# Reading the moving operand of the projections in another column order, with the weight buffers 128 bytes further on

## The chip, the cores and the metric

The kernel runs on one core of one Trainium2 chip. The metric is the device time in microseconds (us) of one execution of the whole program; the times shown are medians of several runs.

## The reference

One decoder block on x of 2048 rows by 1024 columns, float32. A row norm gives h; h times a 1024 x 7680 matrix gives every branch's input. One branch is a gated 31-tap depthwise convolution with a layer norm, the other a sliding-window attention (16 query heads, 4 key/value heads of 64, window 128, a sink per head). Each branch has its own gate and output matrix; two sigmoid gates merge them; a last matrix, the residual and a row norm follow.

```python
h = rmsnorm(x, norm_g[l])
proj = jnp.einsum("bsd,de->bse", h, w_in[l])
glu_in, conv_gate, q, k, v, attn_gate, merge_logits = jnp.split(proj, SPLIT_POINTS, axis=-1)
c = conformer_conv(glu_in, conv_dw_w[l], conv_dw_b[l], conv_ln_g[l], conv_ln_b[l])
y_conv = jnp.einsum("bsc,cd->bsd", c * jax.nn.silu(conv_gate), w_conv_out[l])
...
a = sliding_window_attention(q, k, v, attn_sinks[l])
y_attn = jnp.einsum("bsa,ad->bsd", a * jax.nn.silu(attn_gate), w_attn_out[l])
merged = g_conv * y_conv + g_attn * y_attn
x = x + jnp.einsum("bsd,de->bse", merged, w_out[l])
return rmsnorm(x, final_norm_g)
```

## The kernel before

The sequence is worked through in two sweeps of 1024 rows (`T`), each in two halves of 512 (`TH`). In the projections the weights stand still in TensorE and the activations move: a weight block is 1024 x 128, kept as eight tiles of 128 x 128 (`KC` = 8), and a moving tile is 128 partitions x 512 columns, one half of the rows. Each float32 operand is kept as two parts, a rounded high part and the remainder, and a product is three matmuls into the same PSUM bank: high x high, high weight x low activation, low weight x high activation. `product` (lines 299 to 302) issues these three for one of the eight tiles; `project` (line 307) calls it for two halves and eight tiles, so a weight block makes 2 x 8 x 3 = 48 matmuls. Each is issued with its own weight load (128 x 128, shown as PEld), which runs beside the matmul before it.

A sweep has 76 such blocks: 16 for the gated convolution's input (`gb`, `ga`), 8 for q, 2 for k, 2 for v, 32 for the four gates (`ag`, `cg`, `ma`, `mc`), 8 for the attention's output (`ya`) and 8 for the convolution's (`yc`). Between them, in an order that the kernel itself writes out by a running estimate of TensorE's time (class `Line`; `MM_US` is its price of a matmul), lie the small matmuls of the attention: scores (`sc`, line 799), transposes (`tpp`, line 834) and the products with v (`ov`, line 858), 64 blocks of each. Two matmul sums for the layer norm (`lnmu`, `lnvar`, line 918) use a constant matrix `ones` as weights. The last product with `w_out` (`o`, line 1199) does not go through `product`: there the activations stand still and the weights move.

TensorE runs its instructions in that written order; VectorE (DVE), ScalarE (ACT) and GpSimd (POOL) each run theirs in program order. SyncE (SP) issues all DMAs.

Where the operands lie in SBUF matters for what is changed. In each partition the constants come first, then `slots`, a row of named buffers of 4096 bytes (three of them 4608) made by `slot` (line 82), then `stage`, the buffers of 2048 bytes for raw weights and for their high and low parts (`whi`, `wlo`; lines 262 and 274 to 275), then `work`. The moving tiles `hT`, `aT`, `uT` and `u` are slots. A slot gets its place when it is first used, and `a12` is used last of all. In the program before, every slot and every stage buffer starts at a multiple of 512 bytes, so each weight tile row (128 x 4 = 512 bytes) and each moving row (512 x 4 = 2048 bytes) does too. The matrix `ones` starts 224 bytes behind such a multiple, and the moving tiles of `lnmu` and `lnvar`, which are `work` buffers, 96 bytes behind one. The first two weight blocks of all lie in slots, not in `stage` (`home`, line 409).

Of the kernel before, what the change touches and what calls it, by code (L numbers as in the profile page):

```python
# [19 lines left out]
P = 128  # L20
S = 2048
D = 1024
KC = D // P
# [31 lines left out]
def hybrid_block(ctx: ExitStack, tc: tile.TileContext, x, xt, par_d, w_in, w_conv, sinks, w_attn, w_out,  # L55
                 fin_g, rope_t, out):
    nc = tc.nc
    pe, act, dve, pool = nc.tensor, nc.scalar, nc.vector, nc.gpsimd
# [21 lines left out]
    WIDE = {"c6", "c7", "a14"}  # L80

    def slot(tag, shape, dt, name):
        n = int(np.prod(shape[1:]))
        full = 1024 + P if tag in WIDE else 1024
        t = slots.tile([P, full], dt, tag=tag, name=name)
        v = t[:, 0:n]
        if len(shape) == 3:
            v = v.rearrange("p (a b) -> p a b", b=shape[2])
        elif len(shape) == 4:
            v = v.rearrange("p (a b c) -> p a b c", b=shape[2], c=shape[3])  # L90
        return v
# [20 lines left out]
    ident_r = const.tile([P, P], F32R, name="ident_r")  # L112
    ident = f(ident_r)
    ident_0 = slot(A[4], [P, P], F32, "ident_0")
    make_identity(nc, ident_0)
    dve.tensor_copy(out=ident_r, in_=ident_0)
    ones_0 = slot(A[5], [P, P], F32, "ones_0")
    dve.memset(ones_0, 1.0 / D)
    ones = const.tile([P, P], F32R, name="ones")
# [146 lines left out]
    def load_w(src, name, home=None, steps=None, raws=None):  # L266
# [29 lines left out]

        return lambda k: (parts[k // 4][0][:, k % 4, :], parts[k // 4][1][:, k % 4, :]), keep

    def product(ps, w, r, k, order=(0, 1, 2)):
        parts = ((w[0], r[:, 0, :]), (w[0], r[:, 1, :]), (w[1], r[:, 0, :]))  # L300
        for i, (a, b) in enumerate(parts[n] for n in order):
            pe.matmul(out=ps, lhsT=a, rhs=b, start=(k == 0 and i == 0), stop=(k == KC - 1 and i == 2))  # L302

    def small_bank(name):
        return tp_ps.tile([P, 4, P], F32, tag="tp", name=name).rearrange("p a b -> p (a b)")
# [1 line left out]
    def project(src, rhs, name, evac, halves=(0, 1), small=False):  # L307

        got = {}

        def early():
            got["raws"] = [fetch_raw(src, name, kh) for kh in range(2)]

        def prefetch():
            got["w"] = load_w(src, name, raws=got.get("raws"))

        prefetch.early = early

        def blocks():
            for half in halves:  # L320
                if small:
                    ps = small_bank(f"mm_{name}{half}")
                else:
                    ps = mm_ps.tile([P, TH], F32, tag="mm", name=f"mm_{name}{half}")
                for k in range(KC):
                    product(ps, got["w"][0](k), rhs(k, half), k)
                    if k == KC - 1:
                        with tc.high_priority(offset=PRIO):
                            evac(half, ps)
                    if half == halves[-1] and k % 4 == 3:  # L330
                        got["w"][1](k // 4)
                    yield 3 * MM_US

        return prefetch, blocks, (src, name, evac)
# [8 lines left out]
    def make_tiles(tags, half, name):  # L343
        return [slot(tags[half * 8 + k], [P, 2, TH], F32R, f"{name}{half}_{k}") for k in range(KC)]
# [46 lines left out]
    def opening(items):  # L391
# [58 lines left out]
        def first_blocks():  # L450
            for half in range(2):
                for i in range(2):
                    name = f"mm_{parts[i][1]}0{half}"
                    ps[i, half] = (small_bank(name) if half and i else
                                   mm_ps.tile([P, TH], F32, tag="mm", name=name))
                for k in range(KC):
                    scaled_split(u[half][k], raw[half][k], k)
                    for i in range(2):
                        product(ps[i, half], ws[i][0](k), u[half][k], k, (0, 2, 1))
                        yield 3 * MM_US  # L460
            squares(0)
# [9 lines left out]
        def later(i, half):  # L471
            def blocks():
                name = f"mm_{parts[i][1]}0{half}"
                b = small_bank(name) if half == 0 else mm_ps.tile([P, TH], F32, tag="mm", name=name)
                for k in range(KC):
                    product(b, ws[i][0](k), u[half][k], k)
                    yield 3 * MM_US
                    if i == 2 and k == (2, 4)[half]:
                        yield spread(half)
                        if half == 0:  # L480
                            squares(1)
                        if half:
                            for j in range(2):
                                for kh in range(2):
                                    ws[j][1](kh)
                leave(i, half, b)
                if half:
                    for kh in range(2):
                        ws[i][1](kh)
                if half == 0 and i == 3:  # L490
                    ht[0] = make_tiles(h_tags[0], 0, "hT0_")
                    for k in range(KC):
                        put_h(ht[0][k], raw[0][k], rs[:, 0], k)
                if half == 1 and i == 2:
                    ht[1] = make_tiles(h_tags[0], 1, "hT0_")
                    for k in range(KC):
                        put_h(ht[1][k], raw[1][k], rs[:, 1], k)

            return blocks
# [777 lines left out]
```

## Time and profile before

| what | value |
|---|---|
| median of 3 runs | 1992.11 us (1991.31 to 1993.75) |
| the profiled execution: its own time | 1991.75 us |
| its span, first to last instruction | 1990.0 us |
| mean granted TensorE clock | 0.999 |
| TensorE matmuls (PE) | 1976.9 us busy, 9264 of them |
| weight loads (PEld) | 1649.1 us, 9264 |
| VectorE, ScalarE, GpSimd | 1309.2, 982.7, 429.9 us |
| DMA | 386.13 MB, mean 194 GB/s |

Read the busy time of PE with care: matmuls overlap one another in the records (one of 512 columns is shown with 389 ns, yet the next begins earlier than that), so the distance from start to start tells what one costs. The chain of work that ended last does this sum: each of its pieces is a run of instructions with its length and count, and length divided by count is the time of one.

### The profile page before, as it was taken

To read this page: it belongs to the slowest core of one execution; us is meant where nothing else is said; L and a number is where in the kernel's file an instruction comes from. 1 tells how busy PE (TensorE), PEld (TensorE's weight loads), DVE (VectorE), ACT (ScalarE), POOL (GpSimd) and SP (SyncE) were. 2 spreads that over 40 slices of the span, in tenths; PEclk is the share of its full clock that TensorE was granted. 3 is DMA by queue.
4 is the path that set the end of the run, shared out by engine and by line. 5 is a ranking of instruction groups with operands and counts; after the bars stand their busy time and mean duration, and the time that the engine had idled before them with its cause. 6 is when DMAs were issued, how large, how long until landed. Compare 5 with 4: busy or idle time off the path is not lost.

```text
span 1990.0 us, 27146 instructions
## 1 busy us (share of the span) xinstructions
PE 1976.9 (99%) x9264; PEld 1649.1 (83%) x9264; DVE 1309.2 (66%) x1737; ACT 982.7 (49%) x2250; POOL 429.9 (22%) x462
## 2 busy tenths in 40 slices
PE   8999999999999999999999999999999999999998
PEld 7888888888888888888888888888888888888887
DVE  7998588787888557143857756877787775432424
ACT  7322577556555347244523126775565554553422
POOL 0445323323333323341011121111101100001200
PEclk9999999999999999999999999999999999999999
DMA  8557755665656855356646575556655677553632
GB/s 309 190 185 217 243 180 174 204 187 182 199 188 207 260 192 183 128 193 244 210 151 230 174 232 171 187 187 190 195 179 170 210 233 263 171 185 132 217 122 85
DMA packets 287545, 386.13 MB, mean 194 GB/s; under 512 B 22960, under 2 KB 138032, under 8 KB 287408
## 3 DMA queue, kind: packets, MB, share of 16 engines
q1 hardware_dynamic: 287408, 384.41, 58.8%
q8 instruction: 73, 1.20, 0.2%
q14 instruction: 64, 0.52, 0.1%
HBM read 252.20 MB, written 132.12 MB: 193 GB/s over the span
## 4 chain that ended last, share of the span: by engine, by line
PE 91%; DVE 0%; ACT 0%; POOL 0%; issue 0%
PE mm_cg L302 9%; PE mm_ma L302 9%; PE mm_ag L302 9%; PE mm_mc L302 9%; PE o L1199 9%; PE mm_ya L302 9%; PE mm_yc L302 9%; PE mm_ga L302 8%; PE mm_gb L302 8%; PE sc L799 3%; PE mm_q_b L302 2%; PE ov L858 2%; PE mm_q_a L302 2%; PE tpp L834 1%; PE mm_v L302 1%; PE mm_kb L302 1%
## 5 line engine op out<-in xcount | busy, mean ns | idle before, releaser
L536 DVE SCALAR_TENSOR_TENSOR acc<-glu,par,acc 128x1024 f32<-128x1024 f32 x464 | 595.8, 1284 | 7.4
L1199 PE MATMUL o<-wo,mT 128*128 128x512 f32 x768 | 174.8, 389 | 0.0
L1199 PEld LDWEIGHTS o<-wo,mT 128*128 128x128 f32 x768 | 144.2, 188 | 30.0
L302 PE MATMUL mm_cg<-hT,whi_cg 128*128 128x512 f32 x512 | 160.0, 394 | 0.0
L302 PE MATMUL mm_ma<-hT,whi_ma 128*128 128x512 f32 x512 | 160.0, 393 | 0.0
L302 PE MATMUL mm_ag<-hT,whi_ag 128*128 128x512 f32 x512 | 159.6, 393 | 0.0
L302 PE MATMUL mm_mc<-hT,whi_mc 128*128 128x512 f32 x512 | 158.3, 390 | 0.0
L302 PE MATMUL mm_ya<-aT,whi_ya 128*128 128x512 f32 x512 | 157.7, 389 | 0.0
L302 PE MATMUL mm_yc<-uT,whi_yc 128*128 128x512 f32 x512 | 157.7, 389 | 0.0
L302 PE MATMUL mm_ga<-hT,whi_ga 128*128 128x512 f32 x448 | 139.6, 393 | 0.0
L302 PE MATMUL mm_gb<-hT,whi_gb 128*128 128x512 f32 x448 | 139.5, 392 | 0.0
L822 ACT ACTIVATE ss<-ss,st 128x129 f32<-128x129 f32 x256 | 100.2, 394 | 56.6 <-DVE st L819 56.3
L847 POOL TENSOR_SCALAR_AFFINE_SELECT pc<-pt 64x512 fp32r<-64x512 f32 x128 | 83.7, 654 | 157.7 <-ACT pt L842 138.7
L302 PEld LDWEIGHTS mm_ya<-aT,whi_ya 128*128 128x128 f32 x512 | 96.1, 188 | 20.0
L302 PEld LDWEIGHTS mm_yc<-uT,whi_yc 128*128 128x128 f32 x512 | 96.1, 188 | 19.9
L302 PEld LDWEIGHTS mm_mc<-hT,whi_mc 128*128 128x128 f32 x512 | 95.4, 188 | 19.4
L259 DVE TENSOR_TENSOR pt<-tpp,pt 128x512 fp32r<-128x512 f32 x64 | 44.3, 692 | 99.4 <-ACT pt L842 99.3
L302 PEld LDWEIGHTS mm_ag<-hT,whi_ag 128*128 128x128 f32 x512 | 93.5, 188 | 17.6
L302 PEld LDWEIGHTS mm_ma<-hT,whi_ma 128*128 128x128 f32 x512 | 93.1, 188 | 17.2
L302 PEld LDWEIGHTS mm_cg<-hT,whi_cg 128*128 128x128 f32 x512 | 93.0, 188 | 17.1
L302 PE MATMUL mm_cg<-hT,wlo_cg 128*128 128x512 f32 x256 | 100.0, 391 | 0.0
L302 PE MATMUL mm_ma<-hT,wlo_ma 128*128 128x512 f32 x256 | 100.0, 391 | 0.0
(450 smaller groups left out, 4252.8 us busy)
## 6 DMA issues: line engine op xcount, KB each, us to landing
qk<-d_q SPq DMA_DIRECT2D x64, 256.0 KB, 4.3
d_a<-ss SPq DMA_DIRECT2D x64, 256.0 KB, 3.8
aT<-d_a SPq DMA_DIRECT2D x32, 512.0 KB, 5.9
qk<-d_k SPq DMA_DIRECT2D x60, 256.0 KB, 4.5
d_k<-hlk SPq DMA_DIRECT2D x16, 512.0 KB, 4.7
d_q<-hq_c SPq DMA_DIRECT2D x16, 512.0 KB, 4.6
raw_ag<-in_w_in_dram SPq DMA_DIRECT2D x32, 256.0 KB, 3.9
d_ag<-ag SPq DMA_DIRECT2D x32, 256.0 KB, 3.0
```

The lines of the kernel that those rows point to most:

```text
L259: return eng.tensor_tensor(out=out_, in0=full, in1=f(hi), op=ALU.subtract)
L302: pe.matmul(out=ps, lhsT=a, rhs=b, start=(k == 0 and i == 0), stop=(k == KC - 1 and i == 2))
L536: od(dve.scalar_tensor_tensor(out=to, in0=glu[c][:, j:j + T], scalar=tap(c, j), in1=acc[c], op0=ALU.mult, op1=ALU.add))
L799: pe.matmul(out=scs[qh][:, hp, c0:3 * HD], lhsT=w, rhs=k[:, qh + c0 // HD:qh + 3, j, :], start=(j == 0), stop=(j == 1))
L822: od(act.activation(out=ext[:, h, :], in_=ext[:, h, :], func=AF.Exp, bias=ngm[:, h:h + 1], accum_out=den[:, h:h + 1]))
L834: pe.transpose(out=tpp[:, h, :], in_=sb[:, h, :], identity=ident)
L847: pool.affine_select(out=pc[at], in_=f(pt[0:HD, a]), pattern=[[0, 2 * GQ], [1, HD]], compare_op=ALU.is_ge, fill=0.0, base=0, channel_multi ...
L858: pe.matmul(out=ov[:, cols], lhsT=vv, rhs=pp, start=(i == 0), stop=(i == len(seq) - 1))
L1199: pe.matmul(out=ps, lhsT=a[:, c0:c0 + P], rhs=r, start=(k == 0 and i == 0), stop=(k == KC - 1 and i == 2))
```

## The change

In `product` the moving operand and the output are both read through `swept`, which turns the 512 columns of a row into four rows of 128 columns (512 bytes), each in eight pieces of 16 columns (64 bytes), and walks them piece by piece: columns 0 to 15 of each of the four rows, then columns 16 to 31 of each, and so on. Output and input use the same order, so column c of the input still ends in column c of the output; number, size and order of the matmuls stay.

The slot `a12` becomes 128 bytes longer (32 float32). As it is the last of the slots, the slots all keep their place, and the `stage` and `work` buffers behind them begin 128 bytes further on.

```diff
     def slot(tag, shape, dt, name):
         n = int(np.prod(shape[1:]))
-        full = 1024 + P if tag in WIDE else 1024
+        full = 1024 + P if tag in WIDE else 1024 + (32 if tag == "a12" else 0)
         t = slots.tile([P, full], dt, tag=tag, name=name)
...
+    def swept(ap):
+        return ap.rearrange("p (r b e) -> p b r e", b=8, e=16)
+
     def product(ps, w, r, k, order=(0, 1, 2)):
         parts = ((w[0], r[:, 0, :]), (w[0], r[:, 1, :]), (w[1], r[:, 0, :]))
         for i, (a, b) in enumerate(parts[n] for n in order):
-            pe.matmul(out=ps, lhsT=a, rhs=b, start=(k == 0 and i == 0), stop=(k == KC - 1 and i == 2))
+            pe.matmul(out=swept(ps), lhsT=a, rhs=swept(b), start=(k == 0 and i == 0), stop=(k == KC - 1 and i == 2))
```

## The prediction

> **What bounds the kernel now.** I read the page's sums first, then the chain that ended last, then the waits of TensorE, and last the order of single instructions.
>
> ```profile
> span 1990.0 us, 27146 instructions
> PE 1976.9 (99%) x9264; PEld 1649.1 (83%) x9264; DVE 1309.2 (66%) x1737; ACT 982.7 (49%) x2250; POOL 429.9 (22%) x462
> PEclk9999999999999999999999999999999999999999
> PE 91%; DVE 0%; ACT 0%; POOL 0%; issue 0%
> ```
>
> ```profile
> PE mm_gb L302 <- ACT u_c L377: 5.7, 1, 5.7
> PE mm_q_b L302 <- DVE ra_q__0_1573 L614: 0.4, 1, 0.4
> ```
>
> TensorE is never out of work after the opening: all waits for other engines that its view of waits lists are 6.1 us, and the granted clock is at full in every slice. So the time is the sum of start-to-start distances of 9264 matmuls, and only a shorter distance, or a new wait, changes it. The chain of work gives these distances (start, length, what, count):
>
> ```profile
> 186.83 10.88 PE mm_ag L302 x48
> 821.97 87.04 PE mm_yc L302 x384
> 1896.16 87.05 PE o L1199 x384
> ```
>
> 87.04 / 384 and 10.88 / 48 are both 226.7 ns for a matmul of 512 columns, in three different stages. How much of this is columns and how much a fixed part? Shorter matmuls tell (the chain again, in the stretch 640 to 652 us and 630 to 640 us):
>
> ```profile
> 644.80 0.44 PE tpp L834 x4
> 645.23 2.08 PE mm_mc L302 x9
> 647.32 0.71 PE ov L858 x6
> ...
> 630.86 2.77 PE mm_ma L302 x12
> 633.63 0.71 PE ov L858 x6
> 634.34 2.75 PE mm_ma L302 x12
> ```
>
> `ov` has 256 columns and takes 0.71 / 6 = 118.3 ns; the timeline below has single ones of 120. Twice that less 226.7 is a fixed part of 10.0 to 13.3 ns, and 0.417 to 0.423 ns a column. `tpp` has 128 columns, some 54 ns at that rate, but takes 0.44 / 4 = 110 ns; so there the weight load sets the pace: 128 weight columns, at most 110 ns, 0.86 ns each. Taking 64 bytes, 16 elements, as the piece, a matmul is done with one in 6.7 ns and a load in 13.7.
>
> Is the fixed part tied to the weight load that runs beside it? The timeline, matmuls and then loads (start, length, instruction):
>
> ```profile
> 829.96 0.62 PE L302 MATMUL mm_yc<-uT,whi_yc 128*128 128x512 f32 x2
> 830.42 0.39 PE L302 MATMUL mm_yc<-uT,wlo_yc 128*128 128x512 f32 x1
> 830.64 0.62 PE L302 MATMUL mm_yc<-uT,whi_yc 128*128 128x512 f32 x2
> ...
> 829.97 0.19 PEld L302 LDWEIGHTS mm_yc<-uT,whi_yc 128*128 128x128 f32 x1
> 830.19 0.19 PEld L302 LDWEIGHTS mm_yc<-uT,wlo_yc 128*128 128x128 f32 x1
> 830.42 0.41 PEld L302 LDWEIGHTS mm_yc<-uT,whi_yc 128*128 128x128 f32 x2
> ...
> 647.74 0.28 PE L858 MATMUL ov<-pc,vb 128*128 128x256 f32 x1
> 647.86 0.40 PE L302 MATMUL mm_mc<-hT,whi_mc 128*128 128x512 f32 x1
> ```
>
> The matmuls start at 829.96, 830.19 (the second of the pair) and 830.42; the loads at 829.97, 830.19 and 830.42: each load begins within 0.01 us of a matmul and so reads SBUF beside its first half, always at the same phase. And the distance does depend on where the operands lie:
>
> ```profile
> 685.82 2.95 PE mm_mc L302 x13
> 688.77 0.93 PE lnmu L918 x4
> 689.71 2.31 PE mm_mc L302 x10
> ```
>
> The `lnmu` matmuls have 512 columns and a load each like the others, but `ones` starts 224 bytes and their moving tile 96 bytes behind a multiple of 512. They take 0.93 / 4 = 233 ns, and the ten behind them 231 until the phase has settled again. A pure fixed cost would not know addresses.
>
> **What the change is worth.** It alters no count. I read the fixed part as a collision: the load and the matmul wait for each other when both are in the same eighth (64 bytes) of a 512-byte row. Now the matmul walks a row in 8 x 6.7 = 54 ns and the load in 8 x 13.7 = 110, so during one load the matmul gains one whole round on it and meets it once; a meeting can cost at most the stay of the load in one piece, 13.7 ns, and the fixed part is 10.0 to 13.3. That fits, for 256 columns and for 512 alike, since each has one load.
>
> With `swept` the matmul stays in a piece for 4 x 16 = 64 columns, 27 ns, and moves on four pieces during the load's eight. A load that starts x pieces ahead is x + 4 ahead at its end; it meets nothing if x is 1 to 3 (at 5 to 8 it would run into the matmul from behind, at 0 or 4 it touches it). 128 bytes is x = 2, with one piece of margin either way. Without the shift x would be 0. So both edits are needed, and the price of each alone is not summed.
>
> The terms, on the profiled execution (1990.0 us span, 1.75 around it, 1991.75 in all, 0.36 below the median of the runs):
> - Matmuls with both edits: 76 blocks a sweep, 152 in all, less the two opening blocks whose weights lie in slots, 150 x 48 = 7200. (Row check: the groups of line 302 below have 512 + 256 = 768 for a gate, 16 blocks of 48.) Each loses the fixed part, 10.0 to 13.3; I take the middle, 11.7: 84 us. Ends: 0 (nothing goes) and 96 us.
> - The 96 of the opening: sweep without shift, 0; ends +-13.7 ns each, +-1.3 us.
> - Behind each of the 64 x 3 attention pieces the chain has runs of 9 to 12 at 229 to 231 ns (2.75 / 12, 2.08 / 9). Their surplus of some 3 ns on perhaps 1500 matmuls, 4 us, should go with the collisions; the first matmul of each run waits for a load that the short ones left behind and gains nothing, 192 x 11.7 = 2 us less. Both together: 2 us more gain, ends -2 and +4.
> - The breaks between runs of 64 bytes, 32 in a matmul, on the reading and the PSUM side. No row shows a pattern that short. The nearest are the scores, which move runs of 64 columns, but they take the load's time, so they only bound it from far off: I take 0, because a whole column's time per break, 32 x 0.42 = 13.4 ns, would be the most that a simple restart of one address costs; ends 0 and +96 us.
> - Lines 799, 834, 858, 918 and 1199 keep their column order. Only `work` moves, which gives the 60 or so matmuls that read it another phase: 0, ends +-0.8 us (60 x 13.7 ns).
>
> ```profile
> L302 PE MATMUL mm_cg<-hT,whi_cg 128*128 128x512 f32 x512 | 160.0, 394 | 0.0
> L302 PE MATMUL mm_cg<-hT,wlo_cg 128*128 128x512 f32 x256 | 100.0, 391 | 0.0
> ```
>
> **What comes late next.** With TensorE 5% faster the others must follow (stages of 49.75 us: length, PE, PEld, DVE, ACT, POOL, clock, DMA share, GB/s):
>
> ```profile
> 49.75:99.50 49.75, 49.75 (x227) 41.25 (x226) 48.80 (x63) 19.35 (x37) 23.65 (x18) 1.00 0.53 190
> 99.50:149.25 49.75, 49.75 (x223) 41.20 (x222) 47.52 (x55) 11.90 (x24) 20.36 (x17) 1.00 0.55 185
> 348.25:398.00 49.75, 49.75 (x248) 41.87 (x248) 39.22 (x57) 27.78 (x84) 18.36 (x23) 1.00 0.63 204
> 646.75:696.50 49.75, 49.75 (x231) 41.44 (x230) 28.21 (x33) 18.38 (x36) 15.21 (x12) 1.00 0.86 260
> ```
>
> In the first two stages VectorE works 96.3 of 99.5 us; TensorE would shorten them by 450 x 11.7 = 5.3, VectorE allows 3.2. I charge 3 us there (0 to 5), since q's evacuations at lines 614 and 620 stand in that queue. Elsewhere VectorE has 20% to spare, and DMA 14% in its fullest stage; TensorE's waits there are hidden now and I charge nothing.
>
> Sum: 1991.75 - 84 - 2 + 3 = 1908.75, said as 1909.
>
> [...] The loads start with the matmuls and the distance depends on addresses (rows above). [...] No row here shows a broken PSUM pattern. [...]
>
> **The rivals.**
> 1. No collision is removed: the 10 to 13 ns belong to swapping weights, and order and place change nothing. For it: the same 226.7 in all settled stages. Against it: 233 ns with other addresses. Time 1992.
> 2. Slower by breaks: each of the 32 breaks costs TensorE time. It decides from 11.7 / 32 = 0.37 ns a break, just under one column; at two columns (0.84 ns) it costs 26.9 - 11.7 = 15 ns on 7296 matmuls, +111 us: 2103. For it: no row shows such short runs at full rate. Against: scores with runs of 64 show nothing unusual.
> 3. Slower by direction: weights are read from the far end of a row. Then matmul and load approach each other; stepping both through the eight pieces with the shift gives two meetings a load instead of one fixed part, up to 2 x 13.7 - 11.7 = 16 ns, half of it if they share: +4 to +16 ns, 2020 to 2105. The trace shows starts and lengths of loads, not their direction, so nothing in it excludes this.
>
> **How the numbers follow.** The forecast 0.70 (address-dependent distances and a meeting's price that comes out right); rival 1: 0.11; rival 2: 0.09; rival 3: 0.10. A measurement of this kernel can tell 0.2%, 4 us, from no change. Faster 0.70, same 0.11, slower 0.19. The forecast's own range is 1882 (13.3 ns on each of the 7200, 4 us from the disturbed runs, and 10 more if these too lose all of their surplus, no new wait: 1991.75 - 96 - 4 - 10) to 1955 (under half the collisions go); to leave out no more than 2 in 10 the whole range goes on to rival 1, up to 1996.
>
> **What would show it.** Right: the settled runs of line 302 in the chain at 213 to 217 ns, in `yc` 384 in 82 to 83 us; `o` still at 226.7; `lnmu` still above 226; VectorE above 95% in the first stages and a few waits of TensorE for line 614. Wrong: `yc` at 226.7 (rival 1), or above it with `o` unchanged (2 or 3); 2 would be there with the sweep whatever the shift, 3 would turn to a gain with the shift the other way. A gain in `yc` that the total doesn't show would mean new waits.

## The result: 2.7% slower, and the profile after

| | before | after |
|---|---|---|
| median of 4 runs each | 1991.8 us (1991.31 to 1993.75) | 2045.52 us (2044.98 to 2047.01) |
| ratio | | 1.0269, 95% interval 1.0251 to 1.0287 |
| profiled execution: own time, span | 1991.75, 1990.0 us | 2044.98, 2043.3 us |

The forecast was 1909 us, with a range of 1882 to 1996. The time went the other way and lies outside the range. The page of the kernel after, its sums, its clock and its chain by engine:

```profile
span 2043.3 us, 27164 instructions
PE 2031.0 (99%) x9264; PEld 1651.2 (81%) x9264; DVE 1307.2 (64%) x1737; ACT 984.8 (48%) x2250; POOL 432.9 (21%) x462
PEclk9999999999999999999999999999999999999999
PE 99%; DMA 0%; ACT 0%; DVE 0%; SPq 0%; issue 0%; ACTq 0%
```

The counts, the clock (0.999 before, 1.0 after) and the work of the other engines are as before, and TensorE's only wait that its view of waits lists is the one of the opening:

```profile
PE mm_gb L305 <- ACT u_c L380: 5.5, 1, 5.5
```

So again the time is a sum of distances from matmul to matmul. The chain of the kernel after (start, length, what, count; `product` is now line 305, `o` line 1202, `lnmu` line 921):

```profile
694.83 12.73 PE mm_mc L305 x54
707.55 0.93 PE lnmu L921 x4
...
1103.31 11.20 PE mm_q_b L305 x48
...
1858.74 90.61 PE mm_yc L305 x384
1949.36 87.07 PE o L1202 x384
```

`yc` takes 90.61 / 384 = 236.0 ns, where it took 226.7; `mm_q_b` 233.3; `o`, which does not go through `product`, still 226.7; `lnmu` still 233. The loss is 2043.3 - 1990.0 = 53.3 us, or 7.4 ns on each of the 7200 product matmuls whose weights moved. The pieces of the other lines keep their length (8 `sc` take 0.87 us in both chains, 4 `tpp` 0.44, 6 `ov` 0.71, 384 `o` 87.05 and 87.07), so it is in `product` alone.

The same chain from 1024 to 1100 us shows something that a price per address would not give:

```profile
1024.75 10.88 PE mm_gb L305 x48
...
1080.52 0.44 PE tpv L689 x4
1080.95 4.97 PE mm_v L305 x21
...
1086.37 4.89 PE mm_v L305 x21
```

Right behind a run of `o` at 226.7 ns, the blocks with both edits still run at 10.88 / 48 = 226.7 ns. Four short transposes (`tpv`) come between, and from there on the same instruction takes 4.97 / 21 = 236.7 and 4.89 / 21 = 232.9 ns. The same place before the change:

```profile
1058.06 0.44 PE tpv L686 x4
1058.50 4.79 PE mm_v L302 x21
...
1075.10 10.88 PE mm_q_b L302 x48
```

There too the matmuls behind a `tpv` take a little longer (4.79 / 21 = 228.1), but they come back to 226.7. I call such a settled distance a rhythm. Before, every disturbance ends in the rhythm of 226.7; after, it ends in 233.3 or 236.0, and the 226.7 taken over from `o` is lost at the first disturbance. The experiments ask which edit does this, and by what.

### The profile page after: what moved, and what is told of

Read it like the earlier page. It is cut to its first block, busy times and chain, and to the rows that moved or that the text cites. A ratio compares the mean times of both kernels' runs of the same rounds, so it can differ in the third digit from the quotient of the medians.

```text
span 2043.3 us, 27164 instructions
## 1 busy us (share of the span) xinstructions
PE 2031.0 (99%) x9264; PEld 1651.2 (81%) x9264; DVE 1307.2 (64%) x1737; ACT 984.8 (48%) x2250; POOL 432.9 (21%) x462
## 4 chain that ended last, share of the span: by engine, by line
PE 99%; DMA 0%; ACT 0%; DVE 0%; SPq 0%; issue 0%; ACTq 0%
PE mm_gb L305 9%; PE mm_ga L305 9%; PE mm_cg L305 9%; PE mm_ma L305 9%; PE mm_yc L305 9%; PE mm_ya L305 9%; PE mm_ag L305 9%; PE mm_mc L305 9%; PE o L1202 9%; PE mm_q_b L305 4%; PE mm_q_a L305 4%; PE sc L802 3%; PE mm_v L305 2%; PE ov L861 2%; PE tpp L837 1%; PE mm_kb L305 1%
## 5 line engine op out<-in xcount | busy, mean ns | idle before, releaser
L305 PE MATMUL mm_yc<-uT,whi_yc 128*128 128x512 f32 x512 | 162.2, 398 | 0.0
L305 PE MATMUL mm_ya<-aT,whi_ya 128*128 128x512 f32 x512 | 162.2, 398 | 0.0
L1078 DVE TENSOR_TENSOR lmc<-mm_yc,lmc 128x512 f32<-128x512 f32 x32 | 22.1, 691 | 127.5 <-PE mm_yc L305 127.3
L305 PE MATMUL mm_ya<-aT,wlo_ya 128*128 128x512 f32 x256 | 101.8, 398 | 0.0
```

What stands on the lines that cost most here:

```text
L305: pe.matmul(out=swept(ps), lhsT=a, rhs=swept(b), start=(k == 0 and i == 0), stop=(k == KC - 1 and i == 2))
L1078: dve.tensor_tensor(out=g, in0=ps, in1=g, op=ALU.mult)
```

## The experiments

Two theories stood at the start: the price lies in the sweep's many short runs (rival 2), or the collision is there but load and matmul meet from the other side (rival 3). Where no interval is given, the time is that of a single execution.

**One edit alone (e1, e2), and the shift the other way (e3).**

```diff
 e1: only the change in product; full = 1024 for a12, as before
 e2: only  full = 1024 + P if tag in WIDE else 1024 + (32 if tag == "a12" else 0)
 e3: as after, but + (96 if tag == "a12" else 0)
```

> The new column order alone; a12 keeps its old length, so weights start at a multiple of 512 bytes. Far-end theory (a weight load reads its 512-byte row from the far end, so matmul and load approach each other, and the shift sets how often they meet): stepping through the pieces gives one meeting a load instead of two, so 227 to 232 ns per projection matmul (the opening's two unshifted blocks in the changed kernel took 231) and 1992 to 2030 us. Break theory (the 32 breaks in the access pattern cost TensorE time, wherever the weights lie): 236 ns as in the changed kernel, 2045 us. Same-direction theory of the prediction with a lag of the load: somewhere between 214 and 240 ns, no number.

> The 128 bytes alone, old column order. Far-end theory: the old order runs through all eight pieces several times during a load and meets it as often wherever the load starts: 226 to 231 ns, 1990 to 2020 us. Break theory: no breaks, so 226.7 ns and 1992 us within 0.2%. Same-direction theory: one meeting as before, 226.7 ns, 1992 us.

> The new column order with a12 longer by 384 bytes instead of 128, so x = 6 pieces, the same distance the other way round (-128 modulo 512). Far-end theory: the only shift without a meeting: 213 to 218 ns per projection matmul, o unchanged at 226.7, total 1890 to 1925 us, faster than both kernels. Break theory: 236 ns, 2045 us. Same-direction theory: the load ends in the matmul's piece, at least one meeting, 227 to 240 ns, 1995 to 2070 us.

The chains, first of e1, then of e2, then of e3:

```profile
1012.02 11.11 PE mm_gb L305 x48
...
1837.68 88.75 PE mm_yc L305 x384
```

```profile
1013.58 11.15 PE mm_gb L302 x48
...
1841.06 89.24 PE mm_yc L302 x384
```

```profile
1859.73 90.61 PE mm_yc L305 x384
```

Sweep alone: 2021.06 us, ratio 1.0145 (1.0130 to 1.0160), settled at 231.1 ns. Shift alone: 2025.94 us, 1.0171 (1.0154 to 1.0188), 232.4 ns in the second sweep (233.3 in the first). Each edit by itself loses, 29 and 34 us; together they lose 54, less than the sum. The `mm_gb` lines stand right behind a run of `o`: with one edit alone that block is already at 231.5 or 232.3 ns, where with both edits it was still at 226.7. The shift the other way: 2044.77 us, 1.0264 (1.0249 to 1.0280), the very rhythm of the change (236.0). Rival 3 said that this would turn to a gain; it falls. The break theory's 236 ns came out here, but its 236 for the sweep alone and its 226.7 for the shift alone did not; the prediction's own theory, same direction, had 226.7 for the shift alone as well. None of the three fits all three runs.

**Reading or writing (e5, e6).** The sweep is put on one operand only, with no shift. The columns of the product then end in another order, so part of the result is another one; count and size of the work are the same.

```diff
 e5: pe.matmul(out=ps,        lhsT=a, rhs=swept(b), ...
 e6: pe.matmul(out=swept(ps), lhsT=a, rhs=b,        ...
```

> The moving operand is read in the new order, the output written in the old one, no shift; the columns of each product so land in another order than the reference's, which changes the numbers and nothing else. Reading theory (the cost of the sweep comes from the SBUF reads of the moving operand): 231 ns per settled projection matmul as with the whole sweep, 2021 us. Writing theory (it comes from the broken PSUM pattern): 226.7 ns, 1992 us.

> The mirror image of the run before: the moving operand is read in the old order, the output written in the new one, no shift; again the products' columns land in another order. Reading theory: 226.7 ns, 1992 us. Writing theory: 231 ns, 2021 us.

The chain of e5, then of e6:

```profile
1836.32 88.75 PE mm_yc L305 x384
```

```profile
1809.41 87.04 PE mm_yc L305 x384
```

The whole price of the sweep is in reading SBUF (2020.69 us; 231.1 ns). A PSUM pattern of 32 runs of 64 bytes cost nothing here: 1992.05 us beside 1992.35 for the kernel before, 226.7 ns.

**Is there a place without collisions? (e4, e9)** Each group of blocks gets weight buffers of its own place behind a multiple of 512 bytes, with the sweep in e4 and without it in e9. Room for it is made by 512 bytes more in each buffer; for that the constant `causal` moves into a slot and the scratch memory of the DMAs is halved.

```diff
-                hi = stage.tile([P, 4, P], F32R, tag="whi", name=f"whi_{name}{kh}")
-                lo = stage.tile([P, 4, P], F32R, tag="wlo", name=f"wlo_{name}{kh}")
+                hi, lo = (stage_at(tag, F32R, f"{tag}_{name}{kh}", piece_of(name)) for tag in ("whi", "wlo"))
```

> The new column order with another start of the weights in each stage (whi and wlo buffers 512 bytes longer; in pieces of 64 bytes: ya of the first sweep 0, yc of the first 1, ya of the second 2, yc of the second 3, mc of the first 4, mc of the second 5, glu, q, k, v of the second sweep and the gates ag, cg, ma 6, of the first sweep 7; two opening blocks 0). Read from the chain in the undisturbed stretches. Far-end theory: only 6 is free, 213 to 218 ns, 2 is worst at 236, the others 226 to 233. Break theory: 236 in all. Same-direction theory: three neighbouring values free, the other five not.

> The old column order with another start of the weights in each stage, in bytes behind a multiple of 512: ya of the first sweep 64, yc of the first 192, ya of the second 256, yc of the second 32, mc of the first 16, mc of the second 96, early blocks of the second 384, of the first 320, gates ag, cg, ma 448. Settled distances from the chain. Period theory (the place counts modulo 256 bytes, as with the new order): 256 as 0, 226.7 ns; 384 as 128, 232 to 233; 64 and 320 alike, 192 and 448 alike, all above 226.7. Theory that only a common start in phase is cheap: every offset but 256 at 230 to 240 ns. Should any start be under 226.7 ns, it is one for a faster kernel.

The chain of e4: of the first sweep `mm_mc` at 256 bytes, `mm_ya` at 0 and `mm_yc` at 64, then of the second `mm_mc` at 320, `mm_ya` at 128 and `mm_yc` at 192:

```profile
707.85 45.09 PE mm_mc L323 x195
756.64 86.00 PE mm_ya L323 x372
842.64 90.88 PE mm_yc L323 x384
...
1709.48 48.97 PE mm_mc L323 x207
1767.90 89.60 PE mm_ya L323 x384
1857.50 90.86 PE mm_yc L323 x384
```

The chain of e9: `mm_mc` of the first sweep at 16 bytes, `mm_ya` at 64, `mm_yc` at 192; in the second `mm_mc` at 96, `mm_ya` at 256 and `mm_yc` at 32:

```profile
697.83 45.50 PE mm_mc L320 x195
747.06 86.80 PE mm_ya L320 x372
833.86 87.91 PE mm_yc L320 x384
...
1688.25 48.48 PE mm_mc L320 x207
1746.09 87.09 PE mm_ya L320 x384
1833.18 89.59 PE mm_yc L320 x384
```

With the sweep (e4): 231.2 at 0 bytes and 231.2 at 256, 236.7 at 64 and 236.6 at 320, 233.3 at 128, 236.6 at 192. Without (e9): 233.3 at 16 bytes, 233.3 at 64, 228.9 at 192, 234.2 at 96, 233.3 at 32, and 87.09 / 384 = 226.8 at 256. So the place counts, and a shift of 16 bytes is enough to lose (233.3). Places 256 bytes apart give the same distance at 0 and 256 and at 64 and 320 in e4, at 64 and 320 in e9 (its early blocks of the first sweep, 11.20 / 48 = 233.3), and at 0 and 256 in the old order (226.7 in the kernel before, 226.8 in e9); at 128 and 384 e4 has 233.3 and 236.7 (the early blocks of its second sweep), while the kernel after and e3, at the same two places, are alike at 236.0. The period was forecast and came out but for this pair of e4; that every place but 256 would stand at 230 or above was not quite so (228.9 at 192). But no place is below 226.7: the window of three pieces in which nothing would meet is not there. One place does not even fix the rhythm: swept `mm_ya` of the second sweep at 128 bytes runs at 233.3 ns here and at 236.0 after the change. Each place is tried in one or two stages only, so a difference of 3 ns between two places can be one between rhythms; the same holds for the settings of e7, e8, e10 and e11.

**Do load and matmul collide at one place? (e7, e8)** Now the load reads one single column 128 times, and the moving operand reads every other run of its row twice. In e7 the column lies in the runs that are left out, in e8 in those that are read (`e` is the number of columns in a run). The lengths of the runs go by blocks, 16 to 512 bytes; the gates keep ordinary loads, and the early blocks of the first sweep the old order, with the same one column in both runs. Weights and activations are thereby others; the matmuls' count and size stay.

```diff
+SIDE = 1                    (e7; 0 in e8)
...
+        c = SIDE * e
...
+            return t.rearrange("p a b -> p (a b)")[:, c:c + 1].broadcast_to([P, P])
...
+                b = b.rearrange("p (r h e) -> p h r e", h=2, e=e)[:, 0].unsqueeze(1).broadcast_to([P, 2, TH // (2 * e), e])
```

> Measures by itself whether load and matmul collide. The weight load reads one column 128 times and the moving operand reads every other run of its row twice, the column lying in a run that the matmul skips; that leaves out most of the product. Runs of 16 bytes in ya of the first sweep, 32 in yc of the first, 64 in ya of the second, 128 in yc and the early blocks of the second, 256 in mc of the first, 512 in mc of the second; early blocks of the first sweep: old moving order with a one-column load; ag, cg, ma: 64-byte runs with an ordinary load. Bank theory (load and matmul wait for each other when both read the same 64-byte bank, four banks in 256 bytes, as the map's period of 256 bytes suggests): 213 to 217 ns with runs of 64 and 128 bytes, more with 16, 32 and 256. Theory of no collision (a cost of the load's own): the same 224 to 232 ns in all stages, and the same as in the next run.

> As the run before, but the column that the load reads lies in a run that the matmul does read (byte 0 of a 512-byte row). Bank theory: with runs of 64 and 128 bytes slower than the run before by at least 5 ns, 220 to 260. Theory of no collision: as the run before, stage by stage, within 1 ns.

The chains of e7 and of e8: an early block (old order, one-column load), for e7 a gate (runs of 64 bytes, ordinary loads), then of the second sweep `mm_ya` with runs of 64 bytes and `mm_yc` with 128 bytes:

```profile
175.99 10.99 PE mm_q_b L333 x48
186.97 11.51 PE mm_ag L333 x48
...
1768.52 92.80 PE mm_ya L333 x384
1861.32 90.46 PE mm_yc L333 x384
```

```profile
176.78 10.99 PE mm_q_b L333 x48
...
1768.30 93.18 PE mm_ya L333 x384
1861.48 90.45 PE mm_yc L333 x384
```

Apart and together are the same: 241.7 and 242.7 ns, 235.6 and 235.5 ns, 2047.39 and 2047.57 us. The only pair that differs by more than 1 ns, runs of 16 bytes, has the load that stays apart as the slower one (233.3 against 230.7). Of the two theories on record, the one without collisions had this sameness right but not its 224 to 232 ns; the bank theory's 213 to 217 came nowhere. And with the old order a load that stays in one column still leaves 10.99 / 48 = 229.0 ns, so the fixed part does not need a load that walks through the row. With runs of 64 and 128 bytes a meeting in one eighth of a row shows no price here, and the price of short runs needs no walking load beside it: with runs of 64 bytes 241.7 ns with a standing load, 239.8 with a walking one. (What a load that reads one column 128 times really fetches the runs do not show.)

**Does the fixed part belong to the load's reading? (e11)** Loads of 96, 64 or 32 columns in place of 128, in the blocks' middle matmuls; what these leave out is missing in the result.

```diff
-            pe.matmul(out=ps, lhsT=a, rhs=b, ...
+            m, sweep = w[2]
+            m = P if k == 0 and i == 0 or k == KC - 1 and i == 2 else m
+            to = ps[0:m]
...
+            pe.matmul(out=to, lhsT=a[:, 0:m], rhs=b, ...
```

> Loads of fewer than 128 columns in all but the first and last matmul of each sum (the output then has fewer valid rows, so most of the product is left out): 64 columns in ya of the first sweep, 32 in yc of the first, 96 in mc of the first, all in the old order; 64 in ya of the second, 32 in yc of the second, 96 in mc of the second, 128 in the early blocks of the second, all in the new order. Theory that a load takes reading time from the matmul beside it: the extra over 213.3 ns goes with the length: 223.3 at 96, 220 at 64, 216.7 at 32 in the old order; in the new order 226.6, 222.2 and 217.8. Swap theory (a fixed price for each load): 226.7 ns whatever the length in the old order. If the breaks cost by themselves, the new order stays 4.4 ns above the old at every length.

The chain of e11: in old order 96 columns (`mm_mc`), 64 (`mm_ya`) and 32 (`mm_yc`), then swept 96, 64 and 32:

```profile
691.57 44.91 PE mm_mc L321 x195
740.17 85.56 PE mm_ya L321 x372
825.73 88.76 PE mm_yc L321 x384
...
1679.45 48.28 PE mm_mc L321 x207
1737.04 88.53 PE mm_ya L321 x384
1825.57 89.18 PE mm_yc L321 x384
```

230.3, 230.0 and 231.1 ns in old order, 233.2, 230.5 and 232.2 swept. All theories on record miss: reading time had 223, 220 and 217 in the old order, the swap theory 226.7 whatever the length. A quarter of the load takes nothing off; it adds 4. So no reading time of the load comes back as a shorter distance. How large the fixed part is under these 230 ns, out of the rhythm of 226.7, the run can't tell. And the advantage of the old order over the sweep, 4.4 ns at 128 columns, is 2.9 at 96 and 0.5 to 1.1 at 64 and 32.

**How short a run, or how many? (e10)** Several walks through the 512 columns, no shift; number of rows, length of a row, length of a run.

```diff
+MAP = {"home": (1, 1, 512), "ya0": (4, 32, 4), "yc0": (4, 16, 8), "ya1": (4, 4, 32), "yc1": (4, 2, 64),
+       "mc0": (2, 16, 16), "mc1": (8, 4, 16), "early1": (16, 2, 16), "early0": (2, 4, 64), "gates": (4, 8, 16)}
...
+    def walk(ap, shape):
+        n, m, e = shape
+        return ap.rearrange("p (r b e) -> p b r e", r=n, b=m, e=e) if n > 1 else ap
```

> Weights where they were; another column order in each stage, rows x bytes of a run: ya of the first sweep 4 rows of 512 bytes in runs of 16, yc of the first in 32, ya of the second 128, yc of the second 256, gates 64 (the change's); with runs of 64 also 2 rows of 1024 bytes (mc of the first), 8 rows of 256 (mc of the second), 16 rows of 128 (early blocks of the second); early blocks of the first 2 rows in runs of 256. Break theory (each break in the reading costs): the extra over 226.7 ns goes with the number of breaks: 128, 64, 32, 16, 8 breaks, so 18, 9, 4.4, 2.2 and 1.1 ns for runs of 16 to 256 bytes, and 4.4 for every shape with runs of 64. Meeting theory (which pieces are read while a load reads): no such proportion, and the three other shapes with runs of 64 differ from 231 by more than 2 ns.

The chain of e10: 2 rows of 1024 bytes in runs of 64; then 4 rows of 512 bytes in runs of 16 and of 32; then 8 rows of 256 bytes in runs of 64; then again 4 rows of 512, in runs of 128 and of 256:

```profile
654.76 11.52 PE mm_mc L316 x48
...
749.52 99.69 PE mm_ya L316 x372
849.21 88.75 PE mm_yc L316 x384
...
1717.85 49.58 PE mm_mc L316 x207
1776.98 89.60 PE mm_ya L316 x384
1866.58 87.08 PE mm_yc L316 x384
```

In that order 240.0, 268.0, 231.1, 239.5, 233.3 and 226.8 ns, for 32, 128, 64, 32, 16 and 8 runs in a matmul (16 rows of 128 bytes in runs of 64, the early blocks of the second sweep, take 11.52 / 48 = 240.0). The number of breaks doesn't order them: 64 runs cost as much as the change's 32 in e1 (231.1), 16 runs cost more, and 32 runs in two, eight or sixteen rows cost three times what 32 in four rows do. Rival 2's price per break falls, though not its direction. What the meeting theory expected here, no proportion and more than 2 ns between the shapes, did come out; e7 and e8, which ask for the meeting itself, speak against it. Runs of 256 bytes cost nothing here (226.8 ns).

**Weights' place, or place relative to the moving operand? (e12, e13)** By then open: what the shift's 6 ns hang on. In e12 a constant tile of 128 bytes moves slots and weights together; in e13 the weights are brought back to a multiple of 512 bytes by 384 more. The order is the old one.

```diff
 both:
+    dve.memset(const.tile([P, 32], F32, name="pad"), 0.0)
 e13 as well:
-        full = 1024 + P if tag in WIDE else 1024
+        full = 1024 + P if tag in WIDE else 1024 + (96 if tag == "a12" else 0)
```

> Old column order. A constant tile of 32 floats more stands ahead of all buffers, so that the weight buffers and the moving operands (the row blocks in their slots) both begin 128 bytes behind a multiple of 512: each 128 bytes on, their relative place as before the change. If the 6 ns that the shift costs a matmul come from the place of the weights relative to the moving operand, the settled runs stand at 226.7 ns and the time is 1992 us (1988 to 1996). If they come from the weights' own place in a 512-byte row, they stand at 232.4 to 233.3 ns and the time is 2026 us (2020 to 2032), as with the shift alone.

> Old column order. As the kernel with both places moved, but the weight buffers are padded by 96 floats more, so that they begin at a multiple of 512 bytes again and only the moving operands lie 128 bytes on. If the relative place decides, the settled runs stand at 232.4 to 234 ns and the time is 2026 us (2018 to 2035), though the weights lie where they lay before the change. If the weights' own place decides, they stand at 226.7 ns and the time is 1992 us (1988 to 1996). Both above 230 ns would mean that each operand's own place counts.

The chain of e12, then of e13:

```profile
1807.93 87.04 PE mm_yc L303 x384
```

```profile
1841.38 89.24 PE mm_yc L303 x384
```

Both moved: 1990.58 us, ratio 0.9994 (0.9985 to 1.0004), 226.7 ns. Only the moving operand moved: 2025.82 us, 1.0170 (1.0153 to 1.0187), 232.4 ns, the same piece of 89.24 us as with the weights alone moved. So the relative place decides here, not the weights' own. The `work` buffers are no rival: they begin 128 bytes further on in e2, which loses, and in e12, which doesn't, and at their old place in e13, which loses, and in the kernel before.

## Why the prediction was wrong, point by point

**What held.** TensorE is the bound throughout, no new wait came, `o` stayed at 226.7 ns and `lnmu` at 233, and all of the difference is in the product matmuls. That addresses act on the distance is shown by e2 (232.4 ns), e9 (226.8 to 234.2), e12 (226.7) and e13 (232.4). VectorE's share in the stages from 51 to 153 us is still 98.56 of 102.2 us, but the 3 us that I charged there were never put to the test, since TensorE became slower.

**The row that the case against rival 1 rested on** was misread, though its conclusion holds. The shift moves the moving tiles of `lnmu` from 96 to 224 bytes behind a multiple of 512, the place of `ones`, in the kernel after and in e12 alike. If the relative place made the 233 ns, they should have gone. The chain of e12, then of the kernel before with the six `mm_mc` ahead of `lnmu`, at their ordinary place:

```profile
688.40 0.94 PE lnmu L919 x4
```

```profile
1663.42 1.39 PE mm_mc L302 x6
```

At the same place as `ones`, `lnmu` takes 0.94 / 4 = 235 ns, and six ordinary `mm_mc` take 1.39 / 6 = 232. So a run of four to six between others has not settled, and its 233 ns are no price of an address. "A pure fixed cost would not know addresses" had no row behind it; e2 was the first run that showed it (232.4 against 226.7 ns).

**The step that failed** is "I read the fixed part as a collision", and with it the term of 7200 x 11.7 = 84 us. The profiled execution became 53.3 us longer, 7.4 ns more a matmul where 11.7 less stood. I had a fixed part of 10 to 13 ns and what I took for a dependence on addresses of 6 ns, and made one cause of them because a meeting's price, 13.7 ns, happened to fit the first; that fit proved to be chance. No run shows the term: the piece of 64 bytes was a choice of mine, and the 0.86 ns of a load's column, from which the 13.7 come, an estimate from the 110 ns of `tpp`. What the runs show in its place: load and matmul in one run of 64 or 128 bytes or in different ones take the same (e7 and e8, 241.7 and 242.7 ns, 235.6 and 235.5), and nothing that was tried brought a settled product matmul below 226.7 ns, not the load's place (e4, e9), its length (e11) or the order of the walk (e10). What place and order do comes on top of it: 5.7 ns for the shift, 4.4 for the sweep, 9.3 for both. So 226.7 was the end of the scale and not its middle. The rows said so before: all settled product stages stood at 226.7, the unsettled ones above it, none below. The lower end of the first term should have been a loss, not 0; those unsettled rows, at 2.4 to 6.3 ns more (229.1 to 233 ns), would have given some 17 to 45 us as an estimate of it.

**The window "x is 1 to 3"** followed from the same picture. In e4 every piece from 0 to 448 bytes settled at 231 to 237 ns.

**The breaks at 0.** The value taken was wrong, its end of +96 us was not. The reading side cost 4.4 ns a matmul at the change's walk (e5), and up to 41 in runs of 16 bytes (268.0, e10); the writing side cost nothing, as charged (226.7, e6). The bound that I gave, a column's time per break, 0.42 ns, was an assumption of mine; it held in every shape of e10 (13.3 / 32 = 0.42 is the most); below it the price does not go by the count, so no row gave me a reason to take 0.

**Matmuls behind the attention pieces**, 2 us more gain: these runs became longer like the others (12.73 / 54 = 235.7 before `lnmu`).

**The rivals.** The result lies between the 2020 and 2105 us of rival 3, but by chance: e3 and e7 with e8 refute its mechanism. Rival 2 had the right sign and "with the sweep whatever the shift" (e1), but not its price per break, nor the shift's own loss. Rival 1 was right that no collision of places is removed, as far as e7 and e8 show (alike to 1 ns with runs of 64 and 128 bytes), and wrong that order and place change nothing (231.1 ns in e1, 232.4 in e2). None of the three had the case that happened, that before the change order and place together already gave the best rhythm seen, which each edit lost.

**What stays open.** Among the settings tried, 226.7 ns was kept past a disturbance only with runs of 256 bytes or more, loads of 128 different columns and weights at the moving operand's place modulo 256 bytes; a stream out of it went into one of several rhythms (228.9 ns in e9 to 268.0 in e10). What picks the rhythm was not tested: that it is what disturbed the stream is a guess from the rows around `tpv`. By what circuit the relative place acts, why a place has more than one rhythm, and what the fixed 10 to 13 ns are, no run here tells. No version faster than the kernel before came out of the study.

## What to carry to other kernels

When every undisturbed stage runs at one distance and every other row lies above it, no row shows that a shorter distance exists, and the rows above price a loss, not a gain. A run of four to six matmuls between others was no test of an address here, since it had not settled (`lnmu` 235 ns in e12 at the place of `ones`, six ordinary `mm_mc` 232). For float32 products of this form, the settings tried here speak for weights and moving operand at the same place modulo 256 bytes (226.7 ns at 0 and 226.8 at 256, 228.9 to 234.2 settled at the other places of e2 and e9), moved together if a buffer has to be added (226.7, e12), and for runs of the moving operand of 256 bytes or longer (226.8 at 256, 231.1 to 268.0 in shorter ones, e10); on the PSUM side 32 runs of 64 bytes were free (226.7, e6). Before a mechanism is built on a price that happens to fit, change one of its quantities alone: a shorter load or one shift would have refuted this one.

## What the runs showed that I had not expected

- Relative place: 16 bytes between weights and moving operand take a settled matmul from 226.7 to 233.3 ns (e9), 128 bytes to 232.4 (e2, e13); 256 bytes, or both moved by 128, leave 226.8 and 226.7.
- A shorter weight load made the stream slower: 226.7 ns with 128 columns, 230.3 with 96, 230.0 with 64, 231.1 with 32 (e11).
- One program, one line of code, weights and moving operand at one relative place, and three settled distances, 226.7, 233.3 and 236.0 ns (the kernel after): four short transposes between were enough to end the first, and four groups of them later the stream had settled at the second.
- Walks of the moving operand: 268.0 ns in runs of 16 bytes, 240.0 in runs of 64 from two rows, 231.1 from four (e1), 239.5 from eight, 226.8 in runs of 256 (the others e10); on the PSUM side 226.7 in runs of 64 (e6).
